# Batch-norm matmul on one core: four one-word-per-row reads of the weight at the head of SyncE's queue

## The chip, the core and the metric

The kernel runs on one core of a Trainium2 chip. The metric is the time of one execution on the device in microseconds; the figure for a kernel is the median of its runs. One of the runs of each kernel was also recorded by the hardware profiler, and all views below come from that execution. Engines are named as in the profile: PE (TensorE matmul), PEld (its weight load), DVE (VectorE), ACT (ScalarE), POOL (GpSimd), SP (SyncE).

## What is computed

```python
batch, m, k, n = 16, 512, 1024, 768          # all float32
y = np.matmul(x, weight)                     # (16*512) x 1024  times  1024 x 768
mean = np.mean(y, axis=(0, 1), keepdims=True)
var = np.var(y, axis=(0, 1), keepdims=True)
y_norm = (y - mean) / np.sqrt(var + eps)
return (gamma * y_norm + beta).astype(np.float32)
```

The mean and variance run over all 8192 rows, so no output can be written before the last row of x has gone through the matmul for that column.

## The kernel before

**Tiling.** The 8192 rows of x are 16 chunks of 512 rows (`CH`), each of two quarters of 256 rows (`QR`). The 768 columns are six tiles of 128. The contraction of 1024 is cut into four blocks `jw` with two halves `e` each, so a column tile of one chunk takes 8 matmuls. Products are made in bf16: the transfers that load x and the weight turn f32 into bf16 on their way.

**Loads.** All of x and the weight are loaded by POOL's queue, four transfers for each step. `load_x` (the transfers are line 387) brings rows of x into the tile `ring`; `load_w` (line 378) brings one block `jw` of the weight into `w_sb`: four transfers of 32 partitions, each row of which is two neighbouring rows of the weight, 1536 words. The order is: first quarter of x, block 0 of the weight, second quarter of x, block 1, blocks 2 and 3 together, then the rest of x. POOL's transfers go round eight semaphores: the ninth transfer is issued when the first has landed, and so on.

**Turning x.** DVE turns x (`turn_x`, lines 409 and 416) from `ring` into `xT_sb`, the layout in which PE contracts over the partitions.

**Matmuls.** Column tiles 0 and 1 have x as the stationary operand (`mm_rows`, line 488), the other four have the weight (`mm`, line 553). The first four chunks go through all six column tiles as they arrive; from chunk 4 on only tiles 0 and 1 follow the arrival of x, and the rest is done after the loads have ended. The last two chunks use `ga_unit` (line 793) for tiles 0 and 1. Each unit waits for the turned x that it uses and, in chunk 0, for the weight block that it uses.

**Idle matmuls.** `wake` (lines 569 and 572) lets PE run matmuls on a tile of zeros, `idle_sb`: 8 large and 15 small ones at the very start, and 2 large ones after the first units. They wait for no load. They stand in PE's queue ahead of the first real matmul, so that this one begins when they are over or when its operands are there, whichever is later.

**SP.** SP's queue carries `gamma` and `beta` (`load_affine`, lines 395 and 396: twelve transfers of 128 single words), then the transposing transfers and all stores. Its first entry in the kernel before is the first transfer of `gamma`, which waits for DVE's clearing of that tile.

**Order.** `arrange` simulates the engines and puts the tasks in one fixed order; `seq` ties each instruction to the one before it on its engine. Instructions that are given to `seq` ahead of the task list stand first on their engine.

**Addresses.** `stats` (line 323) holds `(NT - GA) * C + PAD` entries of 24 bytes in each partition, of which the last `PAD` (line 266) are not used; the tiles made after it lie behind it.

Of the kernel before, what the change touches and what calls it, by code (L numbers as in the profile page):

```python
# [227 lines left out]
def kernel(  # L228
# [9 lines left out]
    nc = tc.nc  # L238
    f32 = mybir.dt.float32
# [8 lines left out]
    P = 128  # L248
# [7 lines left out]
    JW = KQ // 64  # L256
# [6 lines left out]
    GA = 2  # L263
    NA = GA * P
    GY = 2
    PAD = 56
    HELD = 1
    ASTAT = {2:tuple(range(4,16))}
    RC = C - 2
# [12 lines left out]
    singles = ctx.enter_context(tc.tile_pool(name="singles", bufs=1))  # L282
# [7 lines left out]
    def seq(bi):  # L290

        ins = bi.ins
        prev = last.get(ins.engine)
        if prev is not None:
            tc.add_manual_dep(
                ins, prev,
                mybir.DependencyInfo(mybir.DependencyClass.NoSync, mybir.DependencyReason.DATA),
                reason="order",
            )
        last[ins.engine] = ins.name  # L300
        return bi
# [20 lines left out]
    tot = singles.tile([P, 2, NA], f32)  # L322
    stats = singles.tile([P, (NT - GA) * C + PAD, 6], f32)
    fin = singles.tile([P, 9 + 6 * len(PIECES)], f32)
# [13 lines left out]
    warm = singles.tile([P, 1], f32)  # L338

    seq(nc.scalar.activation(warm, eps_sb, AF.Sqrt))  # L340


    tasks, turns = [], {}
# [85 lines left out]
    for kind, n, *n1 in order:  # L429
# [21 lines left out]
        for i in range(rows // QR):  # L451
            c, q = divmod(m0 // QR + i, QPC)
# [9 lines left out]
        if rows % QR:  # L462
            t0 = rows // QR * QR // 32
            m1 = m0 + 32 * t0
            c, q = divmod(m1 // QR, QPC)
# [800 lines left out]
    for c, r0, rows in ends:  # L1266
        due = E + 2.0 + 0.6 * c
        n = max(rows // CH, 1)
# [70 lines left out]
```

## Time and profile before

| | us |
|---|---|
| median of 4 runs | 208.29 |
| the four runs | 207.45, 207.78, 208.81, 209.72 |
| the profiled run, its whole time | 207.78 |
| the profiled run, its span | 206.0 |
| PE busy in the span | 192.0 |
| DVE, ACT, POOL busy | 156.7, 139.1, 131.6 |
| first PE instruction, first real matmul in the chain of waits | 1.49, 12.40 |

The span runs from the first to the last instruction that the profiler recorded; 1.78 us of the whole time lie outside it. Times in the views count from the start of the span. The chain of waits is followed back from the last instruction: at each step to what released it, or to the instruction before it on its engine. A transfer's issue and its landing are two things: the issuing engine is done after about half a microsecond, and the data are there some microseconds later.

### The profile page before, as it was taken

The page shows a single profiled execution, that of the slowest core. Times are in us where ns is not written, and L with a number is a line of the kernel's source. Part 1 is how long each engine was busy: PE and PEld are TensorE (multiplying, and loading weights), DVE is VectorE, ACT ScalarE, POOL GpSimd, SP SyncE. Part 2 cuts the span into 40 slices and gives each one's busy share as a digit, 9 for nine tenths or more (in the row PEclk, how much of TensorE's full clock was granted, in tenths as well). Part 3 has the DMA queues.
Part 4 walks back from the last instruction along what each step waited for, and adds up shares of the span by engine and source line. Part 5 has one row for each costly group of instructions (what it writes and reads, how often), then busy time and mean ns, then how long its engine had stood idle before and what let it go on. Part 6 is the DMA issues. An engine that isn't in the chain of part 4 may idle for free.

```text
span 206.0 us, 3483 instructions
## 1 busy us (share of the span) xinstructions
PE 192.0 (93%) x1204; PEld 117.9 (57%) x1219; DVE 156.7 (76%) x238; ACT 139.1 (68%) x248; POOL 131.6 (64%) x148
## 2 busy tenths in 40 slices
PE   7999999999999999999999999999999999996900
PEld 3467564747488888777865444444444445454900
DVE  4220879999999999968989998888999649667800
ACT  2000561369979999998859777997376777676940
POOL 7996954777498999998304998599945440800000
PEclk9999999999999999999999999999999999999675
DMA  5999999999999999999587998999999999997997
GB/s 67 163 195 181 195 196 196 196 198 196 190 193 196 197 197 196 196 197 195 97 105 217 333 338 290 254 356 307 335 264 246 303 322 323 347 345 223 332 347 238
DMA packets 98306, 48.73 MB, mean 237 GB/s; under 512 B 24049, under 2 KB 97777, under 8 KB 98289
## 3 DMA queue, kind: packets, MB, share of 16 engines
q0 software_dynamic: 34688, 18.36, 65.1%
q1 hardware_dynamic: 63600, 30.16, 53.7%
q8 instruction: 9, 0.15, 0.3%
q14 instruction: 9, 0.07, 0.1%
HBM read 36.71 MB, written 25.17 MB: 300 GB/s over the span
## 4 chain that ended last, share of the span: by engine, by line
PE 91%; ACT 3%; DVE 1%; issue 1%; ACTq 0%
PE y_ps L553 53%; PE y_ps L488 24%; PE idle_ps L569 6%; PE y_ps L793 4%; ACT o_sb L1288 3%; PE o_ps L1023 1%; PE a_ps L882 1%; PE y_ps L731 1%; PE o_ps L1053 0%; ACTq L1334 0%; PE idle_ps L572 0%; PE tot_ps L850 0%; DVE idle_sb L313 0%; DVE fin L738 0%; ACT y_sb L741 0%
## 5 line engine op out<-in xcount | busy, mean ns | idle before, releaser
L553 PEld LDWEIGHTS <-w_sb 128*128 128x128 bf16 x512 | 49.6, 97 | 57.2
L553 PE MATMUL y_ps<-x_pl,w_sb 128*128 128x512 bf16 x256 | 59.5, 379 | 0.4
L553 PE MATMUL y_ps<-xT_sb,w_sb 128*128 128x512 bf16 (+1 forms) x241 | 55.1, 377 | 0.4
L387 POOL DMA_DIRECT2D ring<-in_x_dram x76 | 47.4, 629 | 12.5 <-DVE xT_sb L409 5.0
L488 PE MATMUL y_ps<-w_sb,xT_sb 128*128 128x256 bf16 x448 | 50.5, 273 | 0.0
L488 PEld LDWEIGHTS <-xT_sb 128*128 128x128 bf16 x448 | 43.7, 98 | 7.2 <-issue 0.6
L416 DVE STREAM_TRANSPOSE xT_sb<-ring 128x1024 f32<-128x1024 f32 (+1 forms) x29 | 31.2, 1111 | 11.2 <-DMA ring<-in_x_dram 11.1
L689 DVE BATCH_NORM_STATS2 stats<-y_ps 128x6 f32<-128x512 f32 x46 | 30.7, 686 | 10.9 <-PE y_ps L553 9.2
L693 ACT CAST y_sb<-y_ps 128x512 bf16<-128x512 f32 x51 | 29.2, 589 | 14.0 <-DVE stats L689 11.3
L921 POOL TENSOR_TENSOR ring<-ring,sum 128x1024 f32<-128x1024 f32 (+1 forms) x11 | 23.8, 2186 | 14.9 <-DVE ring L916 14.9
L644 POOL TENSOR_TENSOR sum<-sum,sq_sb 128x512 f32<-128x512 f32 x21 | 26.9, 1279 | 3.6 <-ACT sq_sb L637 2.6
L637 ACT ACTIVATE sq_sb<-y_ps 128x512 f32<-128x512 f32 x28 | 16.3, 607 | 18.2 <-PE y_ps L488 17.7
L640 DVE TENSOR_TENSOR sum<-y_ps,sum 128x512 f32<-128x512 f32 x28 | 18.9, 674 | 9.5 <-ACT sq_sb L637 8.2
L525 ACT COPY x_pl<-xT_sb 128x1024 bf16<-128x1024 bf16 x24 | 24.4, 1051 | 1.7 <-DVE xT_sb L416 1.7
L650 ACT CAST y_sb<-y_ps 128x512 bf16<-128x512 f32 x28 | 15.9, 599 | 7.8 <-DVE sum L640 7.5
L525 POOL COPY x_pl<-xT_sb 128x1024 bf16<-128x1024 bf16 x15 | 16.0, 1106 | 8.0 <-DVE x_pl L525 5.2
L916 DVE TENSOR_TENSOR ring<-y_sb,a_ps 128x1024 f32<-128x1024 bf16 (+1 forms) x16 | 16.7, 1078 | 1.0 <-DMA out_dram<-ring 1.0
L1188 ACT CAST ring<-ring 128x1024 f32<-128x1024 bf16 x15 | 15.7, 1050 | 1.9 <-POOL x_pl L525 1.7
L1134 POOL TENSOR_TENSOR ring<-ring,sum 128x1024 f32<-128x1024 f32 x4 | 9.4, 2356 | 7.6 <-DVE ring L1130 7.6
L409 DVE STREAM_TRANSPOSE xT_sb<-ring 128x2048 bf16<-128x2048 bf16 x6 | 13.5, 2289 | 0.3 <-DMA ring<-in_x_dram 0.2
L569 PE MATMUL idle_ps<-idle_sb 128*128 128x512 f32 x20 | 12.0, 758 | 1.5 <-DVE idle_sb L313 1.5
L1023 PE MATMUL o_ps<-ident,y_sb 128*128 128x128 bf16 x104 | 11.3, 249 | 1.7 <-DVE y_sb L1275 1.6
(97 smaller groups left out, 155.3 us busy)
## 6 DMA issues: line engine op xcount, KB each, us to landing
out_dram<-ring SPq DMA_DIRECT2D x38, 512.0 KB, 3.7
ring<-in_x_dram POOLq DMA_DIRECT2D x52, 256.0 KB, 9.0
out_dram<-o_sb SPq DMA_DIRECT2D x6, 512.0 KB, 5.1
ring<-in_x_dram POOLq DMA_DIRECT2D x16, 128.0 KB, 5.3
out_dram<-ring SPq DMA_DIRECT2D x4, 256.0 KB, 2.9
w_sb<-in_weight_dram POOLq DMA_DIRECT2D x8, 96.0 KB, 4.4
w_sb<-in_weight_dram POOLq DMA_DIRECT2D x4, 192.0 KB, 5.1
ring<-in_x_dram POOLq DMA_DIRECT2D x4, 192.0 KB, 8.4
```

Source lines behind the costliest of these rows:

```text
L387: bi = seq(nc.gpsimd.dma_start(x_bf[32 * i:32 * i + 32], src[:, :, KQ * i:KQ * (i + 1)]))
L416: seq(nc.vector.transpose(dst, src[:, :, jw0:jw1]))
L488: seq(nc.tensor.matmul(y_ps[:, s], x_of(c, jw, e, t * P, (t + 1) * P), w_sb[:, jw, e, 0:NA], start=(s == 0 and jw == 0 and e == 0), stop=( ...
L525: seq(nc.scalar.copy(dst, pairs) if eng == "ACT" else ENG[eng].tensor_copy(dst, pairs))
L553: seq(nc.tensor.matmul(y_ps, w_sb[:, jw, e, nt * P:(nt + 1) * P], moving(c, jw, e, q0 * QR, q1 * QR, parted), start=(jw == 0 and e == 0 an ...
L569: seq(nc.tensor.matmul(idle_ps, idle_sb[:, 0:P], idle_sb, start=True, stop=True))
L640: seq(nc.vector.tensor_add(sum1, slot.tile[:, 0:n], sum1))
L644: seq(ENG[eng].tensor_add(acc, acc, state["sq"][:, 0:n]))
L689: seq(nc.vector.bn_stats(dst, slot.tile))
L693: seq(nc.scalar.copy(y(nt, c), slot.tile))
L916: seq(nc.vector.tensor_mul(slot.o, y_row[c].y[:, s0:s1], aff[0][:, None, :].to_broadcast([P, n, NA])))
L921: seq(ENG[eng].tensor_add(slot.o, slot.o, row[:, None, :].to_broadcast([P, n, NA])))
```

## The change

Behind the last instruction of the preparation, SP gets four transfers. Transfer i reads, for the 32 partitions of part i of the weight's block 0, the first word of the 1536 that the partition will get from the real transfer, and writes it into a new tile `touched`, which nothing reads. 128 words are read in all. They wait for nothing and nothing waits for them, but for the end of the program and the later users of the same four semaphores. `PAD` goes from 56 to 54, so that `stats` is 48 bytes shorter.

```diff
-    PAD = 56
+    PAD = 54
...
     seq(nc.scalar.activation(warm, eps_sb, AF.Sqrt))
+    touched = singles.tile([P, 1], f32)
+    first_rows = weight.rearrange("(i jw c e) n -> i jw c (e n)", i=4, jw=JW, e=2)
+    for i in range(4):
+        seq(nc.sync.dma_start(touched[32 * i:32 * i + 32], first_rows[i, 0, :, 0:1]))
```

In the built program the instructions of PE, DVE, ACT and POOL are the same and in the same order; SP has the four transfers ahead of `gamma`, and its transfers go round the eight semaphores four places further on. The tiles for x, the weight and y have the same addresses in both; the small tiles between `stats` and `touched` lie 32 bytes lower.

## The prediction

> **What bounds the kernel now.** I read first the page's chain of waits (shares by engine), then the list of what PE waited for, then the same chain in order of time. The share of PE in the chain:
>
> ```profile
> PE 91%; ACT 3%; DVE 1%; issue 1%; ACTq 0%
> ```
>
> And all that PE waited for in the whole span (total, times, longest, in us):
>
> ```profile
> PE o_ps L1023 <- DVE y_sb L1275: 1.6, 1, 1.6
> PE idle_ps L569 <- DVE idle_sb L313: 1.5, 1, 1.5
> ```
>
> The 1.5 us stand before PE's first instruction, the 1.6 us near 189 us, at the last column's statistics. Between them no wait for a transfer appears. The chain in order of time (start, length) shows what PE does meanwhile at the head, and at the place where the loads are most nearly late:
>
> ```profile
> 1.49 10.07 PE idle_ps L569 x16
> 11.56 0.84 PE idle_ps L572 x15
> 12.40 0.44 PE y_ps L488 x4
> ...
> 84.58 1.46 PE y_ps L553 x6
> 86.03 3.49 PE y_ps L488 x32
> ```
>
> The first real matmul (L488) begins at 12.40 because the idle matmuls end there (11.56 + 0.84), not because an operand came. So the question is how early the operands are. The view of the tile `w_sb`, cut to the four issues of block 0, and the first two turns of x in the timeline:
>
> ```profile
> L378 POOL DMA_DIRECT2D w_sb<-in_weight_dram x4: 489/502/507, 3.7 to 5.2; - x4
> DMA to landing us min/median/max: 4.6/4.6/4.7
> ```
>
> ```profile
> 8.02 1.30 DVE L416 STREAM_TRANSPOSE xT_sb<-ring 128x512 f32<-128x512 f32 x2 [4.89 <-DMA ring<-in_x_dram]
> ```
>
> The last quarter of block 0 is issued at 5.2 and lands at 5.2 + 4.6 = 9.8, which is 12.4 - 9.8 = 2.6 us before its use. The turned x is there at 8.02 + 1.30 = 9.32, 3.1 us before. The block that the change touches is thus early now.
>
> **What the change could repair.** The table of stretches (the last column is GB/s moved, before it the DMA share) has something to repair, off the path:
>
> ```profile
> 5.70:6.30 0.60, 0.60 (x2) 0.34 (x1) 0.00 (x0) 0.00 (x0) 0.60 (x3) 1.00 1.73 168
> 6.30:6.90 0.60, 0.60 (x2) 0.13 (x1) 0.00 (x0) 0.04 (x1) 0.52 (x3) 1.00 0.87 87
> 6.90:7.50 0.60, 0.60 (x2) 0.21 (x1) 0.00 (x0) 0.26 (x1) 0.60 (x2) 1.00 0.88 142
> 7.50:8.10 0.60, 0.60 (x3) 0.32 (x2) 0.08 (x1) 0.00 (x0) 0.43 (x1) 1.00 1.01 190
> 11.70:12.30 0.60, 0.60 (x14) 0.60 (x12) 0.00 (x0) 0.00 (x0) 0.41 (x2) 1.00 1.15 210
> ```
>
> Where block 0 of the weight begins to move, the rate falls to 87 and 142 GB/s and then stands at 190; where block 1 begins (11.70), it is 210 and there is no dip. Something that the first reads of the weight meet is over after a microsecond. Measured against 190 the dip loses 0.6 x (190 - 87)/190 + 0.6 x (190 - 142)/190 = 0.33 + 0.15 = 0.48 us of the load stream. If the four reads take all of it away, block 0 lands at 9.8 - 0.5 = 9.3 and its margin grows from 2.6 to 3.1 us. PE still begins at 12.40: the gain on the path is 0. The cover is the idle matmuls; were they shorter by more than 2.6 us, the 0.48 us would count in full.
>
> **What the four transfers cost.** SP has nothing else to do until `gamma`. The nearest row for issue and landing is `gamma` itself, also single words of SP's queue:
>
> ```profile
> L395 SPq DMA_DIRECT2D gamma_sb<-in_gamma_dram x6: 328/428/496, 48.8 to 54.4; - x6
> DMA to landing us min/median/max: 4.5/4.7/4.7
> ```
>
> Four issues take 4 x 0.43 = 1.7 us, from SP's release at 0.7 to about 2.4; `gamma` follows at 48.8, so nothing of SP is pushed back. By the row the touches land 4.5 to 4.7 us after their issue, from 5.2 to 7.1; that was beside a full stream, while the first four transfers of x at the same head took 3.1 to 4.7 us, so 3.8 to 7.1 is the estimate, about when block 0's packets start (6 us). For the time on the DMA engines there is the view of the stretch from 48 to 60 us, which holds the twelve transfers of `gamma` and `beta`:
>
> ```profile
> q1 hardware_dynamic: 1728, 0.01, 19.5%
> ```
>
> 19.5% of 16 engines over 12 us is 37.4 engine-us for 1728 packets, 21.7 ns each; 1728 is 12 x 144, so a transfer of 128 words makes 128 + 16 packets. A touch of 32 words makes 32 + 16, four make 192, and 192 x 21.7 ns / 16 = 0.26 us on each engine. They run while the first quarter of x moves, so at most x is 0.26 us later: 9.32 becomes 9.58, still 2.8 us early. If the first reads' slow period comes along (0.48 us), 10.06, still 2.3 us early.
>
> Beside the twelve small transfers of `gamma` and `beta` the same stretch moved 193 GB/s, while the page's slices before it show 196: 12 x 3/196 = 0.18 us of stream for twelve, 0.06 for four. So by rows a touch takes between 0.06 and 0.26 us from x; I take 0.26 as the head has no stream yet to hide in.
>
> The Trainium skill speaks against the change, page "DMA: Bandwidth & Descriptors", section "Issuing engines are not separate DMA queues": transfers from different engines run on the same 16 DMA engines and interleave, so that another queue saves only issue time. By it every touch is taken from x in full; by the 193 GB/s most of it is not.
>
> **The other cover, later.** A slip of the load stream at the head could be carried along it, since the loads run at 180 to 198 GB/s in the page's slices up to some 93 us. So I compared each chunk's turn with its use. The closest is at chunk 12:
>
> ```profile
> 84.32 2.37 DVE L416 STREAM_TRANSPOSE xT_sb<-ring 128x1024 f32<-128x1024 f32 x2 [0.21 <-DMA ring<-in_x_dram]
> ```
>
> DVE waited for the transfer; the first of the two turns (half of 2.37) ends at 85.5, and PE uses it at 86.03: 0.5 us of margin. Chunk 13's pair starts at 89.68, is half done at 90.9 and is used at 91.69 (0.8); chunk 14's starts at 95.37 and is used at 97.34 (0.8). So a stream later by 0.26 us is hidden, one later by over 0.5 us is not; a stream earlier by 0.48 us gives PE nothing, as it does not wait.
>
> **The rest.** PE, DVE, ACT and POOL keep their instructions and their order. SP's semaphores are used four places further on, but each transfer still waits for the eighth before it, and the first that waits for a touch does so 45 us after it. The 48 bytes of `stats` are unused padding, and the large tiles do not move. All of this is 0, bounded by the 0.6 us that SP's queue waits at `gamma` for its own landings, which nobody on the path follows.
>
> The sum against the profiled run: span 206.0 + 0 = 206.0, with the 1.78 us outside it 207.78. That run is 0.5 us under the median of the four, which run from 207.45 to 209.72 without any change. For the median after I take 208.2.
>
> **Rivals.**
>
> *The touches push the loads (slower).* The mechanism is one: the words read first meet the slow period one after another, in front of x, and the whole stream slips. It decides from 0.5 us at chunk 12. One slow period after another for the four transfers is 4 x 0.48 = 1.9 us, plus 0.26 on the engines: 2.2 - 0.5 = +1.7 us, 210.0; twice that, 4.3 us, exceeds 3.1 at the head as well and gives +3.8, 212.1. For it: first reads have been seen to stall the stream. Against it: the reads are issued within 1.7 us and go to 16 engines, so the slow period is likely passed once, and x's first data, too, begin only after its issue at 1.3.
>
> *Some of the other runs do wait for the loads (a little faster).* The runs of 208.81 and 209.72 have 1.0 and 1.9 us that the profiled one lacks; if there the stream is late by more than 0.5 us at chunk 12, being 0.48 us earlier takes that much off: the upper runs come down to about 208.3 and 209.2, the median to 208.1, at best to the lowest run, 207.45. For it: the closeness of that margin. Against it: no view shows a wait of this kind, and the spread may be in the stores at the end.
>
> *The touches do not do what they say.* They may land after block 0's packets start, or what is slow may be tied to each row or to POOL's queue. The dip at 6.3 stays; the time is the same, 208.3.
>
> **How the numbers follow.** Hidden either way, with or without the dip: 0.78, time 207.4 to 209.0 (the spread of runs). Other runs helped: 0.10, time 207.4 to 208.1. Loads pushed: 0.12, time 208.8 to 212.1. About 1% (2.1 us) is what a measurement of this kernel can tell from no change. Faster by over 1% means under 206.2, lower than the profiled path allows, as PE's work and its start stay: 0.05, left for what no view shows. Slower by over 1% means over 210.4: the upper part of the third case and some for the unforeseen, 0.09. Within 1%: 0.86. The range 207.2 to 209.4 adds 0.2 and 0.4 us to the first case for the few runs that a median is of, holds the second, and leaves out the larger part of the third.
>
> **What would show it.** Right: the first real matmul in the chain still at 12.4 and no wait of PE for a transfer; the four touches issued between 0.7 and 2.5; the stretch 6.3 to 7.5 above 150 GB/s if the slow period has moved, with a slower start of x around 3 us; the pair of turns of chunk 12 within 0.5 us of 84.3. Wrong: a wait of PE's L488 for DVE or a transfer near 12, 86, 91 or 97 us, or a first matmul after 12.6. A difference over 1% with the same head and loads would mean that something outside the changed instructions, such as the granted clock, decides.

## The result, and the profile after

| | before | after |
|---|---|---|
| median of runs, us | 208.66 (79 runs, 207.45 to 210.17) | 208.18 (52 runs, 207.22 to 209.86) |
| ratio after/before | | 0.9974, 95% interval 0.9963 to 0.9984 |
| profiled run: whole time, span, us | 207.78, 206.0 | 207.97, 206.2 |

The change makes the kernel faster by about a quarter of a percent, 0.5 us. The two profiled runs do not show it: that of before lies 0.9 us under its kernel's median, that of after 0.2 us under its own. Two single profiles cannot be subtracted here; they can be read for what can happen in an execution. Runs over 1.5% above the fastest of their kernel are in a slower state and are left out of the ratios and counts below: four of the kernel before and one of kernel 6. The page's shares of the chain of waits for the changed kernel:

```profile
PE 78%; DMA 10%; ACT 3%; issue 1%; DVE 1%; POOL 1%; ACTq 0%; DVEq 0%; POOLq 0%
```

and what PE waited for in it:

```profile
PE o_ps L1027 <- DVE y_sb L1279: 1.6, 1, 1.6
PE idle_ps L573 <- DVE idle_sb L313: 1.5, 1, 1.5
PE y_ps L492 <- DMA w_sb<-in_weight_dram: 1.0, 1, 1.0
PE y_ps L492 <- DVE xT_sb L420: 0.2, 1, 0.2
```

Transfers were 0% of the chain before and are 10% now, and PE waits 1.0 us for the weight and 0.2 us for turned x (line numbers are four higher than before). The chain in order of time passes through the loads up to 26.78 us:

```profile
2.58 5.02 DMA ring<-in_x_dram
...
13.45 5.71 DMA w_sb<-in_weight_dram
19.17 0.28 issue
19.45 5.90 DMA ring<-in_x_dram
...
25.48 1.25 DVE xT_sb L420
26.73 0.05 issue
26.78 1.92 PE y_ps L492 x16
```

The timeline of PE in the changed kernel has the start, and the places of the two waits:

```profile
1.49 8.84 PE L573 MATMUL idle_ps<-idle_sb 128*128 128x512 f32 x16 [1.49 <-DVE idle_sb L313]
...
11.00 0.60 PE L492 MATMUL y_ps<-w_sb,xT_sb 128*128 128x256 bf16 x4
...
19.30 1.91 PE L492 MATMUL y_ps<-w_sb,xT_sb 128*128 128x256 bf16 x16 [1.04 <-DMA w_sb<-in_weight_dram]
...
26.78 1.92 PE L492 MATMUL y_ps<-w_sb,xT_sb 128*128 128x256 bf16 x16 [0.21 <-DVE xT_sb L420]
```

The wait of 1.04 us is not for block 0, which the change touches, but for the last transfer of blocks 2 and 3, issued at 13.45 and landed at 19.17. In the profile before, the same transfer landed at 18.3, and PE came to these matmuls at 19.48 without a wait:

```profile
19.48 1.75 PE y_ps L488 x16
```

The margin there was 1.2 us, less than the 2.6 us of block 0. In the execution after, PE began 1.2 us earlier (11.00 in the timeline, 12.24 before), which uses the margin up, and the transfer landed 0.9 us later, which makes the wait.

The same idle matmuls that took 10.07 us before took 8.84 here. PE's weight loads tell why: one took 0.34 us up to 6.77 us in the profile before and 0.19 us from 7.54 on; in the profile after the step comes between 4.21 and 5.01:

```profile
4.21 0.34 PEld L573 LDWEIGHTS idle_ps<-idle_sb 128*128 128x128 f32 x1 [0.52 <-issue]
5.01 0.19 PEld L573 LDWEIGHTS idle_ps<-idle_sb 128*128 128x128 f32 x1 [0.47 <-issue]
```

The table of stretches does not show this step: its granted clock reads 1.00 on both sides of it. The clock record of the traces does: its first entry stands at 7.44 us before and at 4.95 us after, where the weight loads change. So PE's full clock is granted at a moment that differs from one execution to the next (between 4.2 and 7.5 us in all fourteen profiles, by the weight loads), and the end of the idle matmuls, my cover, moves by over a microsecond. The Trainium skill has this in "TensorE: Matmul & The Clock Gate", section "Part 1: The HAM clock gate": the clock is decided in windows of about 3.4 us that run freely and do not start with the kernel, so the same kernel gets a different number of slow matmuls in each run. The profiles agree, with steps 2.5 us apart in these two.

The touches and the loads that they precede:

```profile
L344 SPq DMA_DIRECT2D touched<-in_weight_dram x4: 398/412/423, 0.7 to 2.1; - x4
...
DMA to landing us min/median/max: 1.5/2.0/2.7
```

```profile
6.30:6.90 0.60, 0.60 (x3) 0.36 (x2) 0.00 (x0) 0.05 (x1) 0.52 (x3) 1.00 1.04 117
6.90:7.50 0.60, 0.60 (x2) 0.21 (x2) 0.00 (x0) 0.25 (x1) 0.44 (x1) 1.00 0.90 124
```

All four have landed before 5 us, ahead of block 0, and yet the two stretches move 117 and 124 GB/s (87 and 142 before): the slow spell is still there. The view of `w_sb` for the four issues of block 0 says 5.1 us from issue to landing, so the last lands at 5.2 + 5.1 = 10.3 us, 0.5 us later than before and still ahead of the first real matmul.

### The profile page after: what moved, and what is told of

It is laid out like the page before. It is cut to its first block, busy times and chain, and to the rows that moved or that the text cites. A ratio compares the mean times of both kernels' runs of the same rounds, so it can differ in the third digit from the quotient of the medians.

```text
span 206.2 us, 3487 instructions
## 1 busy us (share of the span) xinstructions
PE 190.6 (92%) x1204; PEld 115.5 (56%) x1219; DVE 156.2 (76%) x238; ACT 139.2 (67%) x248; POOL 131.6 (64%) x148
## 4 chain that ended last, share of the span: by engine, by line
PE 78%; DMA 10%; ACT 3%; issue 1%; DVE 1%; POOL 1%; ACTq 0%; DVEq 0%; POOLq 0%
PE y_ps L557 49%; PE y_ps L492 21%; DMA ring<-in_x_dram 7%; PE y_ps L797 4%; ACT o_sb L1292 3%; DMA w_sb<-in_weight_dram 3%; PE o_ps L1027 1%; PE a_ps L886 1%; POOL ring L391 1%; PE y_ps L735 1%; DVE xT_sb L420 1%; PE o_ps L1057 0%; ACTq L1338 0%; PE tot_ps L854 0%; DVE fin L742 0%
## 5 line engine op out<-in xcount | busy, mean ns | idle before, releaser
L644 DVE TENSOR_TENSOR sum<-y_ps,sum 128x512 f32<-128x512 f32 x28 | 18.9, 675 | 8.8 <-ACT sq_sb L641 7.6
L1027 PE MATMUL o_ps<-ident,y_sb 128*128 128x128 bf16 x104 | 10.6, 221 | 1.7 <-DVE y_sb L1279 1.6
L573 PE MATMUL idle_ps<-idle_sb 128*128 128x512 f32 x20 | 10.7, 690 | 1.5 <-DVE idle_sb L313 1.5
```

What stands on the lines that cost most here:

```text
L644: seq(nc.vector.tensor_add(sum1, slot.tile[:, 0:n], sum1))
```

## The experiments

Each was timed in five rounds beside the kernel before, on the chip that its batch ran on (three batches of four). Of the kernel before, 64 of the 97 runs compared took more than 208.6 us; these upper runs are counted as a measure of the spread. Three ideas are told apart: that the place read early counts (the weight theory, or place theory), that any early transfer of SP does, and that the shifted addresses do.

| kernel | median, us | ratio to before, 95% interval | runs over 208.6 |
|---|---|---|---|
| 1: the change again | 208.45 | 0.9990 (0.9964 to 1.0016) | 6 of 12 |
| 2: padding and tile, no transfers | 208.52 | 1.0000 (0.9969 to 1.0031) | 6 of 12 |
| 3: 128 words from x | 208.50 | 0.9980 (0.9955 to 1.0005) | 6 of 12 |
| 4: 512 words, all blocks of the weight | 207.91 | 0.9956 (0.9936 to 0.9976) | 0 of 12 |
| 5: as 4 | 207.82 | 0.9948 (0.9920 to 0.9976) | 1 of 12 |
| 6: 512 words from x | 208.00 | 0.9972 (0.9945 to 1.0000) | 2 of 11 |
| 7: before, 12 idle matmuls | 210.53 | 1.0078 (1.0053 to 1.0104) | |
| 8: as 4, 12 idle matmuls | 210.51 | 1.0078 (1.0052 to 1.0104) | |
| 9: 512 words from gamma | 208.10 | 0.9967 (0.9936 to 0.9999) | 2 of 12 |
| 10: as 9 | 207.89 | 0.9947 (0.9923 to 0.9971) | 0 of 12 |
| 11: as 6 | 208.25 | 0.9965 (0.9936 to 0.9994) | 5 of 12 |
| 12: as 4 | 207.84 | 0.9959 (0.9936 to 0.9982) | 0 of 12 |

**1. The change again.** No edit.

> The changed kernel once more, beside the kernel before on the same chip. Weight theory (the touches take the slow first reads of the weight's block 0 off the load stream, and this pays in executions where PE's clock wakes early and the loads, not the idle matmuls, set the start): ratio 0.9974 again, 0.996 to 0.999. Any-transfer theory (an early transfer of SP is what counts) and address theory (the shorter padding counts): the same ratio. Nothing-there theory: 1.000.

Its interval holds 0.9974 and 1.000: twelve runs cannot see an effect of this size.

**2. The addresses alone.**

```diff
     touched = singles.tile([P, 1], f32)
-    first_rows = weight.rearrange("(i jw c e) n -> i jw c (e n)", i=4, jw=JW, e=2)
-    for i in range(4):
-        seq(nc.sync.dma_start(touched[32 * i:32 * i + 32], first_rows[i, 0, :, 0:1]))
+    assert touched is not None
```

> The padding of 54 and the tile touched, but no transfers. Weight theory and any-transfer theory: 1.000 (0.999 to 1.001). Address theory: 0.997.

1.0000, and as many upper runs as with the change in the same batch. The interval is too wide to exclude 0.9974, so that the addresses have no part in the change's own 0.26% is not shown; it does exclude the 0.9956 of kernel 4 below, which has the same padding. Its stretches, in a kernel without any touch, are more telling:

```profile
6.30:6.90 0.60, 0.60 (x2) 0.19 (x1) 0.00 (x0) 0.02 (x1) 0.52 (x3) 1.00 1.13 125
6.90:7.50 0.60, 0.60 (x3) 0.20 (x2) 0.00 (x0) 0.28 (x1) 0.60 (x2) 1.00 1.13 177
```

The dip at block 0 that I read as the weight's first reads is half gone here by itself (87 and 142 in the profile before, 102 and 92 in that of kernel 7, which has no touch either). In the profile of kernel 1, the same program as the change, it is gone (190 and 169). It comes and goes with the execution.

**3. Elsewhere.**

```diff
-    first_rows = weight.rearrange("(i jw c e) n -> i jw c (e n)", i=4, jw=JW, e=2)
+    first_rows = x_flat[M // 2:M // 2 + 1024].rearrange("(i jw c e) n -> i jw c (e n)", i=4, jw=JW, e=2)
```

> The same four transfers of 32 words with the same steps, read from the middle of x in place of the weight. Weight theory: 1.000 to 1.002, as the slow packets at the start of block 0 stay and x is a little later. Any-transfer theory: 0.997.

0.9980, between the two expectations and compatible with both: inconclusive.

**4, 5 and 12. All blocks of the weight.** Four words for each partition in place of one; `touched` has four columns at the same address.

```diff
-    touched = singles.tile([P, 1], f32)
-    first_rows = weight.rearrange("(i jw c e) n -> i jw c (e n)", i=4, jw=JW, e=2)
+    touched = singles.tile([P, JW], f32)
+    first_rows = weight.rearrange("(i jw c e) n -> i c jw (e n)", i=4, jw=JW, e=2)
     for i in range(4):
-        seq(nc.sync.dma_start(touched[32 * i:32 * i + 32], first_rows[i, 0, :, 0:1]))
+        seq(nc.sync.dma_start(touched[32 * i:32 * i + 32], first_rows[i, :, :, 0]))
```

> Four transfers of 128 words that touch the rows of all four blocks of the weight. Weight theory, if what is slow is tied to the rows: 0.994 to 0.997, better than one block, with no packets over 350 ns in blocks 1 to 3 either. Weight theory, if what is slow is tied to the tensor as a whole: as with one block, 0.9974. Any-transfer theory: 0.997. All: if the 512 words hold x up instead, over 1.000.

> The 512-word touch of all four blocks once more. Weight theory (slow first reads of the weight's rows, spread over all four blocks, delay the loads; executions in which PE would wait for them gain): 0.9956 again, 0.993 to 0.998, and no runs above about 208.6. Chance theory: 0.999 to 1.000, with the upper runs back.

> The 512-word touch of the weight beside the three above, on one chip. Place theory: 0.995, and 0.2 to 0.5% below gamma's. Any-transfer theory: the same as gamma's within 0.1%.

Three times 0.995 to 0.996, and one run of 36 over 208.6. The effect is there; its estimate is larger than the change's, though the intervals overlap. At this point the weight theory looked confirmed; the control with the same number of words from another place was still missing.

**6 and 11. 512 words from x.** The edit of 4 with the middle of x in place of the weight.

> The 512 words read with the same steps from the middle of x. Weight theory: 1.000 (0.998 to 1.002). Any-transfer theory (early reads of SP from anywhere help): 0.9956.

> The 512 words from the middle of x once more. Place theory with the weight alone: 1.000. Place theory in which the 4 MB of x that are touched count too, when they are loaded: 0.997 again. Any-transfer theory: as with gamma and as with the weight, 0.995 to 0.997.

0.9972 and 0.9965, the first with an interval that just reaches 1.000, the second clear of it. Reading x helps too, though with 7 of 23 upper runs against 1 of 36 it is not shown to do as much; and the 4 MB that are touched are loaded later, so the place could still count.

**9 and 10. 512 words from gamma.** This removes that doubt: gamma's 3 KB are read nowhere near the head. Against kernel 4:

```diff
-    first_rows = weight.rearrange("(i jw c e) n -> i c jw (e n)", i=4, jw=JW, e=2)
+    words = gamma.rearrange("(a p) -> p a", a=NT)
     for i in range(4):
-        seq(nc.sync.dma_start(touched[32 * i:32 * i + 32], first_rows[i, :, :, 0]))
+        seq(nc.sync.dma_start(touched[32 * i:32 * i + 32], words[32 * i:32 * i + 32, 0:JW]))
```

> The same four transfers of 128 single words, read from gamma, whose 3 KB lie in one place: an early use of SP's queue and of the DMA engines without a touch of the weight or of x. Place theory (what counts is that the place read later has been read once): 1.000 (0.998 to 1.002), the upper runs above 208.6 as often as before. Any-transfer theory: 0.995 to 0.997.

> The same kernel as the one before it, for twice as many runs: the same expectations.

0.9967 and 0.9947, beside the weight's 0.9959 in the same batch, with 2 of 24 runs over 208.6. Touching neither the weight nor x does as well as touching the weight. The weight theory falls: what is left for the place is at most the 0.2% to which these runs tell the two apart. Where PE stands in kernel 10:

```profile
PE y_ps L492 <- DMA w_sb<-in_weight_dram: 0.5, 1, 0.5
PE a_ps L886 <- ACT y_sb L810: 0.5, 1, 0.5
PE y_ps L492 <- DVE xT_sb L420: 0.2, 1, 0.2
```

It still waits for the loads, 0.7 us in all; and there is another wait of 0.5 us, on ACT, after the loads.

**7 and 8. More idle matmuls.** Do the touches act through the waits for loads at all?

```diff
-    WAKE = 8
+    WAKE = 12
```

> The kernel before with 12 large idle matmuls at the start in place of 8: PE starts 4 x 0.86 = 3.4 us later, after 14.4 us at the earliest. If the idle matmuls alone set the start in every execution: 3.4 us more, ratio 1.0165. If the loads set the pace in most of them: less, as part of it covers waits: 2.2 to 2.9 us, ratio 1.011 to 1.014, and a narrower spread, as the loads' differences are covered.

> The 512-word touch of all blocks with 12 idle matmuls. Weight theory: the loads are covered, so the same time as the kernel before with 12 (within 0.1%). If the touch works in another place than the waits for loads: 0.9956 of it, 0.9 us less.

Without touches the later start costs 1.0078, 1.6 us (1.1 to 2.2 by the interval), about half of the 3.4 us by which the start moved and less than either expectation: the rest replaced time that PE spends waiting or would have been late by anyway. In neither profile does PE wait for a load; of kernel 8:

```profile
PE o_ps L1027 <- DVE y_sb L1279: 1.6, 1, 1.6
PE idle_ps L573 <- DVE idle_sb L313: 1.5, 1, 1.5
```

With the loads covered the touches bring nothing, 1.0078 as well, where 0.9956 would have been 0.9 us less; the two medians differ by 0.02 us, and resampling the ten runs of each gives some 0.5 us to either side. So what they bring comes through waits that a later start takes away. Those seen are mostly waits for loads; the wait on ACT is absent from the profiles of 7 and 8 too, so that it has no part is not shown.

The profiles in which PE waits for nothing between the first real matmul and the last column (before, 5, 6, 7 and 8) give a measure of the waiting: from the start of that matmul in the chain, 12.06 to 15.80 us, to the end of the span they all take 193.4 to 193.6 us. With the 1.78 us outside the span, the latest start in a profile with 8 idle matmuls, 12.40 in that of before, makes 207.8 us without a wait, and 73 of the 79 runs of the kernel before took longer. An estimate of what it would take at the median without waits is the 210.5 of kernels 7 and 8 less 3.4, or 207.1; the kernel before loses about 1.6 us to waits, the one with 512 words about 0.8.

## Why the prediction was right, and where its steps were wrong

The forecast of no change beyond 1%, at 208.2, held (208.18), and its range too. That the two agree to 0.02 us is luck: 208.2 was the median of four runs with no gain, and over 79 runs the kernel before has 208.66, from which the change takes 0.5. Much of the working did not hold.

- **"No wait for a transfer appears", hence "the gain on the path is 0".** This step failed. It was true of the profiled execution of before and I carried it over to all. In that execution the clock came late (7.5 us) and the idle matmuls covered the loads; in the one of after it came at about 5 us and PE waited 1.2 us for loads. Kernel 7 shows that waiting is the rule: 3.4 us of later start cost 1.6. The runs shown, 207.45 to 209.72 around a profile of 207.78, had said that the profile was near the bottom.
- **"Were they shorter by more than 2.6 us".** The cover was read at block 0 and at chunks 12 to 14 only. The waits came between, at 19.30 us for blocks 2 and 3 and at 26.78 for turned x, where the working has no margin; at the first the margin in the profile before was 1.2 us.
- **"Some of the other runs do wait for the loads".** That rival, with a chance of 0.10, is what happens, and gives the sign. Its time, 207.4 to 208.1, is just under the 208.18 measured. Its place, chunk 12, is not where the profiles show waits, and its cause, the stream earlier by the weight's 0.48 us, is not shown by any run.
- **The dip as something "that the first reads of the weight meet".** Wrong: it is half gone (2) or there (7) without touches, it stayed with the change's own and is gone in kernel 1, the same program, and block 0 landed at 10.3, not at 9.3.
- **What the touches take from x.** Not shown: 0.06 to 0.26 us, and 0.74 with a slow spell in front, were worked out; the first turn of x began at 8.48 in place of 8.02, 0.46 us later, but in kernel 1, the same program, at 7.87. Single executions differ by more than the term. The issues took 1.80 us (1.7 worked out). Their landing, 3.1 to 4.7 us from the rows of `gamma` and of x, was mis-sized: 1.5 to 2.7 us.
- **"The touches push the loads".** No run shows the +1.7 us; 512 words did not either.
- **Margins at chunks 12 to 14.** Not tested alone. With PE's start no longer fixed they say only how early the loads were in one execution. In that of kernel 2 the chain goes from the turn of chunk 11, at 79.76 us, straight to PE's matmuls at 81.06: there the margin is nothing, though no wait is listed.

What stays open is why a few hundred words, read early from anywhere, take 0.3 to 0.5% off the time. The profiles, one for each kernel, do not show the loads landing earlier. At the head the stretch from 3 to 9 us moved 155 and 150 GB/s without touches, 149 with the change, 152 with kernel 4 and 152 with kernel 10. The slow spell moves towards the start (from 3.0 to 4.5 us the rate is 148 and 131 without, and 94 with kernel 4), and the total stays. The last transfer of blocks 2 and 3, the one that PE waited for, landed at 18.3 (before), 19.4 (2) and 18.6 us (7) without touches, at 18.9 to 19.3 with 128 words and at 18.3 to 19.0 with 512: one execution of each kernel does not tell these apart. Whether 512 words do more than 128 is not settled either: within one batch 0.9956 stands against 0.9990 and 0.9980, but the change's own 52 runs give 0.9974. Whether the number of words or of transfers counts, and whether the part that `touched` plays could be taken by another early use of SP's queue, was not tried.

Reading four words for each partition (kernel 4) is the fastest kernel found, 207.8 to 207.9 us in each of three batches; the same from gamma, 207.9 and 208.1, is not told from it.

## What to carry to other kernels

Where a kernel hides its loads behind a warm-up on a clock that is granted at a varying moment, a single profile can show either of two regimes: look at where the profiled run lies among the runs before saying that nothing waits. When a transfer is meant to warm a place, try the same transfer on a place that has no part in the loads: here the control did as well as the idea. An effect of 0.3% took 52 and 79 runs to see here; 12 runs did it only with a larger dose of the cause.

## What the runs showed that was not expected

Single early words help from each of the three places tried, as said. Beside that, the end of PE's slow clock alone moved the first real matmul from 12.24 us (before) to 10.83 (kernel 10). And there is a second source of spread, after the loads: PE waited 0.3 to 0.6 us on ACT at L886, where scale and shift are spread over PSUM, in the profiles of kernels 1, 3, 9, 10, 11 and 12 and not in the others; it appears with words from the weight, from x and from gamma, and kernels 4 and 12, which are the same program, differ in it.
